# Four projections at 512 weight columns in two halves of rows, and the scan's multiplication on VectorE

## The chip, the cores and the metric

One Trainium2 chip, one core. The metric is the device time of one execution in microseconds (us). The kernel before took 2485.04 us, the median of 3 runs (2484.7 to 2485.36).

## What is computed

One layer of an encoder, on two groups of tokens with shared weights: the sample group S (512 tokens) and the prompt group R (1024 tokens), width 1024, float32.

```python
u = rmsnorm(x, p['mix_norm_g']) @ p['w_in']
ssd_out = ssd_mixer(u[..., OFF_Z:OFF_XBC], u[..., OFF_XBC:OFF_DT], u[..., OFF_DT:OFF_Q], ...)
att_out = attention_mixer(u[..., OFF_Q:OFF_K], u[..., OFF_K:OFF_V], u[..., OFF_V:IN_COLS], ...)
h = x + jnp.concatenate([ssd_out, att_out], axis=-1) @ p['w_out']
h = h + memory_cross_attention(rmsnorm(h, p['xatt_norm_g']), rmsnorm(mem, p['mem_norm_g']), ...)
hm = rmsnorm(h, p['mlp_norm_g'])
y = h + jnp.square(jax.nn.relu(hm @ p['mlp_w1'])) @ p['mlp_w2']
```

`ssd_mixer` holds two chunked scans (one in each direction, 8 heads of 64, chunks of 128 tokens) behind a convolution and a gate z; `attention_mixer` has three banded patterns over 8 heads; `memory_cross_attention` attends to 256 memory tokens of each group, whose keys and values come from `memn @ wkv`.

## The kernel before

**Dense products.** Activations lie transposed in SBUF, each as a high part and a low part (`chi`, `clo`), and so do the weights (`whi`, `wlo`); a product is three matmuls, hi by hi, hi by lo, lo by hi (`mm3`, L198, so L199 to L201). In the four projections of this change (gate z, query/key/value, the memory's keys and values, w_out) and in the cross attention's query the tokens are the stationary operand (128 x 128) and the weights stream: `proj` (L272) makes one tile of 128 tokens by 256 columns with 8 k-steps of three matmuls, 24 matmuls of 256 columns. The convolution's projection, the MLP and the attention's output projection stream 512 columns.

**Weights.** `load_w` (L179) brings a slab of 128 x 2048 values in four pieces of 256 KB: a DMA to `raw` (4 buffers), a cast on ScalarE to `whi`, and a subtraction to `wlo`, on GpSimd for pieces 0 and 2, on VectorE for 1 and 3. The pool `wp` has three buffers each of `whi` and `wlo`, so a slab can be loaded while two others are in use. `slab` (L194) loads 1024 rows by 256 columns.

**The scan.** `ssd` first runs backward over the chunks, then forward. For a chunk and a group of heads `weigh` (L619) makes four 128 x 128 weight tiles in `se`: ScalarE and VectorE steps for each head (L623 to L626), one exponential over 128 x 512 (L627), and one multiplication of 128 x 512 by the exponentials on GpSimd (L628). `inside` (L631) multiplies on TensorE with these tiles (L635). There are 24 such multiplications, 8 for S and 16 for R.

**Order.** Generators of dense work are woven with one chain of mixers (scan S, attention S, scan R, attention R): `weave` (L1130) lets the mixers take `rate` steps for each yield of the dense work. A scheduler that orders the instructions of each engine then fixes the final order when the program is built; at run time each engine works through its own order and waits by semaphore. PSUM: three banks `mm` for projections (`mm_bank`), two `tp`, three for the mixers.

Of the kernel before, what the change touches and what calls it, by code (L numbers as in the profile page):

```python
# [84 lines left out]
def encoder(ctx: ExitStack, tc: tile.TileContext, I, y_p, y_s):  # L85
# [93 lines left out]
    def load_w(src, a, b):  # L179

        hi = wp.tile([128, a, b], F32R, name="whi")
        lo = wp.tile([128, a, b], F32R, name="wlo")

        for s in range(4):
            raw = wp.tile([128, 2, 256], F32, name="raw", bufs=4)
            sl = slice(s * 2, s * 2 + 2) if a == 8 else slice(0, 2)
            sc = slice(0, 256) if a == 8 else slice(s * 256, s * 256 + 256)
# [84 lines left out]
    def proj(w, quads, t):  # L272
# [6 lines left out]
        return ps  # L279

# [19 lines left out]
    def w_in(st, pool, wx, first=False):  # L300
# [67 lines left out]
        def gates(b):  # L368
            for c in range(2):
                if b == 0:  # L370
                    wz.append(slab(W_IN, OFF_Z + c * 256))
                yield from gate(c, wz[c], range(b * 4, b * 4 + 4, 2))

        def gate(c, w, ts):
            for t in ts:
                th = pool.tile([128, 512], F32, name="ev").rearrange("p (t c) -> p t c", t=2)
                for i in range(2):
                    if i:
                        yield
                    ps = proj(w, at, t + i)  # L380
                    nc.scalar.activation(th[:, i], ps, AF.Tanh, scale=0.5)
                    nc.vector.scalar_tensor_tensor(th[:, i], th[:, i], 1.0, ps, op0=OP.add, op1=OP.mult)  # L382
                dst = st.zs[t * 128:t * 128 + 256, c * 256:c * 256 + 256]
                nc.sync.dma_start(dst.rearrange("(t p) c -> p t c", p=128), th)
                catch_up()
                yield
# [64 lines left out]
    def w_in_qkv(st, pool, rot, mid=None):  # L451
# [7 lines left out]
        def heads(c, t, hl):  # L459

            qk = c // 2
            e, sq = f(hl[1]).rearrange("p (t c) -> p t c", t=2), f(hl[0])
            x = e.rearrange("p t (h e) -> p t h e", h=4)
            x3 = e.rearrange("p t (h e) -> p (t h) e", h=4)
            nc.scalar.activation(sq, e.rearrange("p t c -> p (t c)"), AF.Square)
# [3 lines left out]
            nc.vector.tensor_tensor(x3, x3, r[:, :8, None].to_broadcast([128, 8, 64]), op=OP.mult)  # L469
            t1, t2 = x[..., 0:8], x[..., 8:16]  # L470
            m = sq[:, 0:256].rearrange("p (j t h c) -> p j t h c", j=4, t=2, h=4)
            for j, src in enumerate((t1, t2, t1, t2)):
                w = rot[qk][:, t:t + 2, j, None, :].to_broadcast([128, 2, 4, 8])
                (nc.gpsimd if j % 2 else nc.vector).tensor_tensor(m[:, j], src, w, op=OP.mult)
# [3 lines left out]
        def transposed(c, t, hl):  # L478
            qk = c // 2
            e = f(hl[1]).rearrange("p (t c) -> p t c", t=2)  # L480
            pt = tp_bank()
            for hp in range(2):
                for i in range(2):
                    o = (hp * 2 + i) * 128
                    nc.tensor.transpose(pt[:, o:o + 128], e[:, i, hp * 128:hp * 128 + 128], perm)
# [9 lines left out]
        order = [(c, t) for c in range(4) for t in range(0, nt, 2)]  # L495
        order += [(c, b * 4 + t) for b in range(nt // 4) for c in (4, 5) for t in (0, 2)]
        ws = {}
        for c, t in order:
            if c not in ws:
                ws[c] = slab(W_IN, OFF_Q + c * 256)  # L500
            w = ws[c]
            if mid and (c, t) == (4, 4):
                mid()
            if True:
                hl = [pool.tile([128, 512], F32R, name="ev") for _ in range(2 if c < 4 else 1)]
                e = f(hl[-1]).rearrange("p (t c) -> p t c", t=2)
                for i in range(2):
                    if i:
                        yield
                    ps = proj(w, st.at, t + i)  # L510
                    nc.scalar.copy(e[:, i], ps)
                if behind:
                    transposed(*behind.pop())
                if c < 4:
                    heads(c, t, hl)
                    behind.append((c, t, hl))
                else:
                    for i in range(2):
                        for g in range(2):
                            r0 = 64 + (t + i) * 128 + g * 64  # L520
                            dst = st.vd[r0:r0 + 64, (c - 4) * 256:(c - 3) * 256]
                            nc.sync.dma_start(dst.rearrange("(r j) c -> j r c", r=4), e[g * 64:g * 64 + 64, i, :])
                yield


    def ssd(st, pool):
# [92 lines left out]
        def weigh(c, g, cbm, e):  # L619
# [8 lines left out]
            nc.gpsimd.tensor_tensor(w, w, e[:, 0], op=OP.mult)  # L628
# [254 lines left out]
    def memory(pool, late=None):  # L883
        for c in range(8):
            w = slab(WKV, c * 256)
            if late and c == 4:
                late()
            for st in (S, R):
                need("mem" + st.tag)
                kf = pool.tile([128, 512], F32, name="ev").rearrange("p (m c) -> p m c", m=2)  # L890
                ss = pool.tile([128, 2], F32, name="kss", bufs=2)
                for mt in range(2):
                    if mt:
                        yield
                    ps = proj(w, st.mt[:1], st.mt[1] + mt)
                    nc.scalar.copy(kf[:, mt], ps)
                    if c < 4:
                        nc.scalar.activation(ps, ps, AF.Square, accum_out=ss[:, mt:mt + 1])
                hl = [pool.tile([128, 2, 256], F32R, name="ev") for _ in range(2)]
                if c >= 4:  # L900
                    nc.vector.tensor_copy(hl[0], kf)
                    nc.gpsimd.tensor_tensor(hl[1], kf, f(hl[0]), op=OP.subtract)
                    for j in range(2):
                        nc.sync.dma_start(st.v[:, c - 4, j], f(hl[j]).rearrange("p m c -> p (m c)"))
                    yield
                    continue
                r = rstd(pool, ss, 2, 256)
                pt = tp_bank().rearrange("p (e m) -> p e m", e=2)
                for mt in range(2):
                    nc.vector.tensor_scalar(kf[:, mt], kf[:, mt], r[:, mt:mt + 1], None, op0=OP.mult)  # L910
                    for e in range(2):
# [348 lines left out]
```

## Time and profile before

| what | before |
|---|---|
| median of 3 runs | 2485.04 us |
| the profiled execution, device time | 2483.99 us |
| its span, first to last instruction | 2481.9 us |
| TensorE busy (matmuls) | 2413.2 us, 97% |
| VectorE, ScalarE, GpSimd busy | 1416.4, 977.0, 749.0 us |
| mean granted TensorE clock | 0.986 |

The profiled execution lies 1.05 us under the median of the runs. A busy TensorE is one with a matmul in flight: matmuls overlap, each record being longer than the distance to the next, so the rate is read from starts, not from durations. The granted clock is a share of 2.4 GHz; 0.5 of it is 1.2 GHz. Idle time of another engine costs nothing unless TensorE waits for it.

### The profile page before, as it was taken

Reading aid. Unit: us, or ns where it says so; the run is one execution under the profiler, and the core shown is the slowest. Engines: PE = TensorE matmul, PEld = TensorE weight load, DVE = VectorE, ACT = ScalarE, POOL = GpSimd, SP = SyncE. Lnnn points to the kernel's source line nnn. Section 1 sums busy time; section 2 is a strip of 40 time slices with the busy share of each in tenths; the row PEclk is TensorE's granted clock in tenths of the full one; section 3 lists DMA queues with packets and bytes.
Section 4 is the critical chain, followed back from the end, with each engine's and each line's share of the span. In section 5 each row is a group of like instructions: output and inputs, shape, how many; then the busy total and the mean of one; then the engine's idle time right before and its main releaser. Section 6 shows DMA issues by size and latency. Waiting matters only on the chain.

```text
span 2481.9 us, 38736 instructions
## 1 busy us (share of the span) xinstructions
PE 2413.2 (97%) x14435; PEld 2129.5 (86%) x14435; DVE 1416.4 (57%) x2870; ACT 977.0 (39%) x2393; POOL 749.0 (30%) x612
## 2 busy tenths in 40 slices
PE   8899999999899998999999999999999999999999
PEld 6899789998798997888888899999888888888887
DVE  7676876658866566565655636555634434444344
ACT  6445455545544555444433325333521211212111
POOL 3253313425654212332424212111222222322221
PEclk9999999999899999999999999999999999999999
DMA  5555344547675344335335511111111111111111
GB/s 182 182 191 172 121 138 144 169 135 256 226 256 161 87 124 117 105 107 134 107 95 179 181 45 50 54 52 52 35 44 42 52 52 34 54 49 51 51 34 68
DMA packets 258603, 272.28 MB, mean 110 GB/s; under 512 B 43474, under 2 KB 222960, under 8 KB 258416
## 3 DMA queue, kind: packets, MB, share of 16 engines
q1 hardware_dynamic: 258416, 269.82, 35.2%
q8 instruction: 114, 1.87, 0.3%
q14 instruction: 73, 0.60, 0.1%
HBM read 215.55 MB, written 54.20 MB: 109 GB/s over the span
## 4 chain that ended last, share of the span: by engine, by line
PE 73%; DMA 3%; DVE 3%; issue 1%; ACT 1%; POOL 1%; SPq 0%; ACTq 0%; POOLq 0%; DVEq 0%
PE mm L199 15%; PE mm L201 14%; PE mm L200 14%; PE tp L199 7%; PE tp L200 7%; PE tp L201 7%; PE mc L800 2%; PE ma L771 1%; PE mb L787 1%; PE tp L218 1%; DMA se<-acp 1%; DVE se L626 1%; PE mc L635 0%; DMA ak<-qkp 0%; PE tp L981 0%
## 5 line engine op out<-in xcount | busy, mean ns | idle before, releaser
L191 POOL TENSOR_TENSOR wlo<-raw,whi 128x512 fp32r<-128x512 f32 x240 | 364.9, 1537 | 550.3 <-ACT whi L189 451.2
L199 PE MATMUL mm<-whi,chi 128*128 128x256 f32 x1792 | 521.1, 292 | 2.3 <-DVE ev L382 1.7
L201 PE MATMUL mm<-whi,clo 128*128 128x256 f32 x1792 | 511.6, 288 | 1.3 <-DVE clo L225 1.2
L200 PE MATMUL mm<-wlo,chi 128*128 128x256 f32 x1792 | 511.6, 286 | 0.0
L1112 DVE TENSOR_TENSOR h<-mm,h 128x512 f32<-128x512 f32 x384 | 262.5, 688 | 380.7 <-PE mm L201 380.4
L191 DVE TENSOR_TENSOR wlo<-raw,whi 128x512 fp32r<-128x512 f32 x240 | 296.7, 1250 | 97.1 <-ACT whi L189 96.2
L199 PEld LDWEIGHTS mm<-whi,chi 128*128 128x128 f32 x1792 | 344.6, 192 | 5.0 <-DVE ev L382 2.4
L189 ACT CAST whi<-raw 128x512 fp32r<-128x512 f32 x480 | 265.2, 618 | 203.8 <-PE tp L200 100.3
L200 PEld LDWEIGHTS mm<-wlo,chi 128*128 128x128 f32 x1792 | 344.3, 192 | 0.8
L201 PEld LDWEIGHTS mm<-whi,clo 128*128 128x128 f32 x1792 | 342.2, 192 | 2.3 <-DVE clo L225 2.2
L199 PE MATMUL mm<-whi,hidh 128*128 128x512 f32 x768 | 304.2, 396 | 0.0
L201 PE MATMUL mm<-whi,hidl 128*128 128x512 f32 x768 | 303.1, 395 | 0.0
L200 PE MATMUL mm<-wlo,hidh 128*128 128x512 f32 x768 | 302.6, 394 | 0.0
L200 PE MATMUL tp<-clo,whi 128*128 128x512 f32 x720 | 284.4, 395 | 0.0
L199 PE MATMUL tp<-chi,whi 128*128 128x512 f32 x720 | 284.3, 395 | 0.0
L201 PE MATMUL tp<-chi,wlo 128*128 128x512 f32 x720 | 284.0, 394 | 0.0
L1096 POOL TENSOR_TENSOR hidl<-hr,hidh 128x512 fp32r<-128x512 f32 x96 | 124.6, 1298 | 475.7 <-ACT hidh L1095 302.6
L1095 ACT CAST hidh<-hr 128x512 fp32r<-128x512 f32 x96 | 59.6, 621 | 401.1 <-PE mm L200 325.7
L201 PEld LDWEIGHTS mm<-whi,hidl 128*128 128x128 f32 x768 | 144.4, 188 | 33.6
L200 PEld LDWEIGHTS mm<-wlo,hidh 128*128 128x128 f32 x768 | 144.6, 188 | 32.3
L199 PEld LDWEIGHTS mm<-whi,hidh 128*128 128x128 f32 x768 | 144.5, 188 | 32.2
L201 PEld LDWEIGHTS tp<-chi,wlo 128*128 128x128 f32 x720 | 135.4, 188 | 31.1
(284 smaller groups left out, 4132.7 us busy)
## 6 DMA issues: line engine op xcount, KB each, us to landing
raw<-in_mlp_w_dram SPq DMA_DIRECT2D x256, 256.0 KB
raw<-in_w_in_dram SPq DMA_DIRECT2D x96, 256.0 KB
qkp<-ev SPq DMA_DIRECT2D x32, 256.0 KB
raw<-in_xatt_wkv_dram SPq DMA_DIRECT2D x32, 256.0 KB
se<-acp SPq DMA_DIRECT2D x16, 512.0 KB
raw<-in_w_out_dram SPq DMA_DIRECT2D x32, 256.0 KB
raw<-in_xatt_wq_dram SPq DMA_DIRECT2D x32, 256.0 KB
ak<-qkp SPq DMA_DIRECT2D x32, 256.0 KB
```

Source lines behind the costliest of these rows:

```text
L189: nc.scalar.copy(hi[:, sl, sc], raw)
L191: eng.tensor_tensor(lo[:, sl, sc], raw, f(hi[:, sl, sc]), op=OP.subtract)
L199: nc.tensor.matmul(ps, lh, rh, start=start, stop=False)
L200: nc.tensor.matmul(ps, lh, rl, start=False, stop=False)
L201: nc.tensor.matmul(ps, ll, rh, start=False, stop=stop)
L218: nc.tensor.transpose(pt[:, k, t, :], xn[t][:, (2 * kp + k) * 128:(2 * kp + k + 1) * 128], units(2 * kp + k))
L626: nc.vector.scalar_tensor_tensor(w[:, h], cbm[:, 0, g], col[2], w[:, h], op0=OP.mult, op1=OP.add)
L771: nc.tensor.matmul(pq[:, i, :W], qu, ops[i][0][j], start=j == 0, stop=j == 1)
L800: nc.tensor.matmul(po[:, i * 64:i * 64 + 64], pT[:, i * nk + j, :], ops[i][1][j][:, rs], start=j == 0, stop=j == nk - 1)
L1095: nc.scalar.copy(hh[:, ft], r)
L1096: nc.gpsimd.tensor_tensor(hl[:, ft], r, f(hh[:, ft]), op=OP.subtract)
L1112: nc.vector.tensor_tensor(h[t][:, cs], ps, h[t][:, cs], op=OP.add)
```

## The change

`wide_slab` takes 512 columns at once, as two halves of 512 rows, each a slab of its own in `wp`. `wide_proj` makes two tiles of 128 tokens by 512 columns at a time: both take the four k-steps of one half, then the four of the other, and the next pair of tiles begins with the half that was used last. The evictions of the four projections are rewritten for 512 columns of one tile where there were 256 columns of two. `weigh` multiplies on VectorE, the values' low parts are subtracted on VectorE from PSUM (before: a cast on VectorE and a subtraction on GpSimd). Six rates of `weave` change.

```diff
@@ load_w
+        r, c = {8: (2, 256), 4: (1, 512), 2: (2, 256)}[a]
         for s in range(4):
-            raw = wp.tile([128, 2, 256], F32, name="raw", bufs=4)
+            raw = wp.tile([128, 512], F32, name="raw", bufs=4).rearrange("p (r c) -> p r c", r=r)
...
+    def wide_slab(w, c0):
+
+        src = w[:, c0:c0 + 512].rearrange("(u k p) c -> u p k c", p=128, k=4)
+        return [load_w(src[u], 4, 512) for u in range(2)], [0]
...
+    def wide_proj(w, quads, tiles, each):
+
+
+        halves, last = w
+        for t0 in tiles[::2]:
+            ps = [mm_bank() for _ in range(2)]
+            for n in range(2):
+                u = last[0] if n == 0 else 1 - last[0]
+                wh, wl = halves[u]
+                for i in range(2):
+                    hi, lo = quads[(t0 + i) // 4]
+                    ts = slice((t0 + i) % 4 * 128, (t0 + i) % 4 * 128 + 128)
+                    for k in range(4):
+                        kk = u * 4 + k
+                        mm3(ps[i], hi[:, kk, ts], lo[:, kk, ts], wh[:, k, :], wl[:, k, :],
+                            n == 0 and k == 0, n == 1 and k == 3)
+                    if n == 1:
+                        each(t0 + i, ps[i])
+                    yield
+            last[0] = 1 - last[0]
...
+        def gate(t, ps):
+            th = pool.tile([128, 512], F32, name="ev")
+            nc.scalar.activation(th, ps, AF.Tanh, scale=0.5)
+            nc.vector.scalar_tensor_tensor(th, th, 1.0, ps, op0=OP.add, op1=OP.mult)
+            nc.sync.dma_start(st.zs[t * 128:t * 128 + 128, :], th)
...
-                dst = st.qk[qk, (c % 2) * 2:(c % 2) * 2 + 2, j, :, t * 128:t * 128 + 256]
-                nc.sync.dma_start(dst.rearrange("h p t -> p h t"), f(hl[j]).rearrange("p (h t) -> p h t", h=2))
+                dst = st.qk[qk, :, j, :, t * 128:t * 128 + 128]
+                nc.sync.dma_start(dst.rearrange("h p t -> p h t"), f(hl[j]).rearrange("p (h t) -> p h t", h=4))
...
+        for part, each in enumerate((query_key(0), query_key(1), value)):
+            w = wide_slab(W_IN, OFF_Q + part * 512)
+            for b in range(nt // 4):
+                if mid and part == 2 and b == 1:
+                    mid()
+                yield from wide_proj(w, st.at, range(b * 4, b * 4 + 4), each)
@@ weigh
-            nc.gpsimd.tensor_tensor(w, w, e[:, 0], op=OP.mult)
+            nc.vector.tensor_tensor(w, w, e[:, 0], op=OP.mult)
@@ memory
+        def values(st, c, t, ps):
+            hl = [pool.tile([128, 512], F32R, name="ev") for _ in range(2)]
+            nc.scalar.copy(hl[0], ps)
+            nc.vector.tensor_tensor(hl[1], ps, f(hl[0]), op=OP.subtract)
...
-                if c >= 4:
-                    nc.vector.tensor_copy(hl[0], kf)
-                    nc.gpsimd.tensor_tensor(hl[1], kf, f(hl[0]), op=OP.subtract)
@@ w_out
+        for c in range(2):
+            w = wide_slab(W_OUT, c * 512)
+            cs = slice(c * 512, c * 512 + 512)
+            for pr in range(st.nt // 2):
+                need("mix%d%s" % (pr, st.tag))
+                yield from wide_proj(w, st.mixT, range(pr * 2, pr * 2 + 2), each)
@@ the weaving
-        weave(mixing, 0.3, marked(w_in_qkv(S, pool, rot), "qkv s"))
+        weave(mixing, 0.4, marked(w_in_qkv(S, pool, rot), "qkv s"))
-        weave(mixing, 0.45, marked(w_in(R, pool, wx), "w_in p"), 1.0)
+        weave(mixing, 0.5, marked(w_in(R, pool, wx), "w_in p"), 1.0)
-        weave(mixing, 0.9, marked(w_in_qkv(R, pool, rot, memories), "qkv p"), 1.0)
+        weave(mixing, 1.0, marked(w_in_qkv(R, pool, rot, memories), "qkv p"), 1.0)
-        weave(mixing, 0.6, chain(S, (atA,), hp, tp_only), 2.0)
+        weave(mixing, 0.7, chain(S, (atA,), hp, tp_only), 2.0)
-            weave(mixing, 0.65, mlp(S, hid, ready))
+            weave(mixing, 0.5, mlp(S, hid, ready))
```

How this moves instructions, in the order of two engines. TensorE at the first columns of w_out for S, before: the end of one tile of tokens (`mm_8948`) and the beginning of the next (`mm_8974`) on one slab (`whi_8930`, `wlo_8931`).

```order
L199 MATMUL mm_8948<-whi_8930,chi_8103 128x256
L200 MATMUL mm_8948<-wlo_8931,chi_8103 128x256
L201 MATMUL mm_8948<-whi_8930,clo_8104 128x256
L199 MATMUL mm_8974<-whi_8930,chi_8103 128x256
L200 MATMUL mm_8974<-wlo_8931,chi_8103 128x256
L201 MATMUL mm_8974<-whi_8930,clo_8104 128x256
```

And now: the second tile (`mm_7413`) ends with the first half of the rows (`whi_7376`), and the first tile (`mm_7412`) takes the second half (`whi_7394`).

```order
L205 MATMUL mm_7413<-whi_7376,chi_6799 128x512
L206 MATMUL mm_7413<-wlo_7377,chi_6799 128x512
L207 MATMUL mm_7413<-whi_7376,clo_6800 128x512
L205 MATMUL mm_7412<-whi_7394,chi_6799 128x512
L206 MATMUL mm_7412<-wlo_7395,chi_6799 128x512
L207 MATMUL mm_7412<-whi_7394,clo_6800 128x512
```

The matmuls of 512 columns stand where there were two of 256, and an accumulation stays open over both halves.

GpSimd before, from the scan of R beside the loading of w_out's slabs (`wlo_9273`): the multiplication of `se` (L628) stands in one queue with the subtractions of the weights (L191) and of the memory's values (L902).

```order
L647 TENSOR_TENSOR sy_8725<-sy_8725,syo_8792 128x512
L628 TENSOR_TENSOR se_8740<-se_8740 128x512
L628 TENSOR_TENSOR se_8786<-se_8786 128x512
L902 TENSOR_TENSOR ev_8859<-ev_8804,ev_8858 128x512
L191 TENSOR_TENSOR wlo_9273<-raw_9274,whi_9272 128x512
```

VectorE now, at the same stage (scan of R, `wlo_7395` is the second half of w_out's first columns):

```order
L638 SCALAR_TENSOR_TENSOR se_6848<-scbm_6845,dtp_2636,se_6848 128x128 x4
L707 TENSOR_SCALAR sy_6774<-sy_6774,rsr_6966 128x512
L640 TENSOR_TENSOR se_6848<-se_6848 128x512
L192 TENSOR_TENSOR wlo_7395<-raw_7400,whi_7394 128x512
L192 TENSOR_TENSOR wlo_7395<-raw_7408,whi_7394 128x512
L231 SCALAR_TENSOR_TENSOR clo_6800<-tp_7281,cols_81,chi_6799 128x256
```

The multiplication (L640) has moved into VectorE's queue, ahead of w_out's subtractions.

## Rows read from the trace of the kernel before

**Rows 1.** The page: span, busy time by engine, 40 slices.

```profile
PE 2413.2 (97%) x14435; PEld 2129.5 (86%) x14435; DVE 1416.4 (57%) x2870; ACT 977.0 (39%) x2393; POOL 749.0 (30%) x612
...
PE   8899999999899998999999999999999999999999
...
DVE  7676876658866566565655636555634434444344
```

**Rows 2.** TensorE timeline near 1660 us, 256 columns: first and last of 43 rows.

```profile
1659.31 0.28 PE L201 MATMUL mm<-whi,clo 128*128 128x256 f32 x1
...
1664.35 0.29 PE L201 MATMUL mm<-whi,clo 128*128 128x256 f32 x1
```

**Rows 3.** TensorE timeline near 2300 us, 512 columns: first and last of 61 rows.

```profile
2289.84 0.40 PE L200 MATMUL tp<-clo,whi 128*128 128x512 f32 x1
...
2303.79 0.39 PE L200 MATMUL mm<-wlo,hidh 128*128 128x512 f32 x1
```

**Rows 4.** Groups of TensorE by shape: xcount | busy us, mean ns | idle before, releaser.

```profile
L200 PE MATMUL mm<-wlo,chi 128*128 128x256 f32 x1792 | 511.6, 286 | 0.0
```

**Rows 5.** Stretches: length, busy PE PEld DVE ACT POOL, clock, DMA share, GB/s.

```profile
571.00:684.00 113.00, 98.27 (x684) 92.16 (x682) 100.78 (x202) 67.75 (x204) 69.13 (x57) 0.91 0.71 232
684.00:724.00 40.00, 40.00 (x338) 39.85 (x337) 23.34 (x40) 16.99 (x42) 23.13 (x17) 1.00 0.69 228
```

**Rows 6.** Waits of TensorE in 571 to 684 us: total, times, longest.

```profile
PE mc L635 <- POOL se L628: 9.7, 4, 4.3
PE tp L912 <- DVE ev L910: 3.0, 3, 1.1
```

**Rows 7.** Groups of VectorE and GpSimd in 571 to 684 us.

```profile
L626 DVE SCALAR_TENSOR_TENSOR se<-scbm,dtp,se 128x128 f32<-128x128 f32 x44 | 21.2, 534 | 0.4 <-ACT se L625 0.4
L624 DVE SCALAR_TENSOR_TENSOR se<-se,sa 128x128 f32<-128x128 f32 x41 | 17.2, 470 | 2.4 <-ACT se L623 2.4
L191 DVE TENSOR_TENSOR wlo<-raw,whi 128x512 fp32r<-128x512 f32 x10 | 11.8, 1208 | 2.3 <-ACT whi L189 2.1
L575 DVE TENSOR_TENSOR sxs<-sx,sdd 128x512 f32<-128x512 f32 x9 | 6.7, 749 | 0.0
...
L628 POOL TENSOR_TENSOR se<-se 128x512 f32<-128x512 f32 x11 | 14.8, 1342 | 14.2 <-ACT se L625 3.8 <-issue 3.7 <-ACT se L627 2.9
```

**Rows 8.** VectorE and GpSimd timelines around the longest of these waits.

```profile
663.12 5.29 POOL L191 TENSOR_TENSOR wlo<-raw,whi 128x512 fp32r<-128x512 f32 x2 [1.70 <-ACT whi L189]
668.37 1.31 POOL L628 TENSOR_TENSOR se<-se 128x512 f32<-128x512 f32 x1
...
665.92 4.42 DVE L626 SCALAR_TENSOR_TENSOR se<-scbm,dtp,se 128x128 f32<-128x128 f32 x5
```

**Rows 9.** All uses of `se`: duration ns min/median/max, first and last start.

```profile
L626 DVE SCALAR_TENSOR_TENSOR se<-scbm,dtp,se x64: 335/342/1389, 580.8 to 761.3; 128x128 f32<-128x128 f32 x64
```

**Rows 10.** VectorE and GpSimd over the span: the values' steps, and a like subtraction from PSUM.

```profile
L901 DVE CAST ev<-ev 128x512 fp32r<-128x512 f32 x8 | 5.9, 732 | 2.9 <-DMA vp<-ev 1.4 <-ACT ev L896 1.1 <-issue 0.3
L984 DVE TENSOR_TENSOR xqT<-tp,xqT 128x512 fp32r<-128x512 f32 x24 | 16.4, 683 | 3.8 <-ACT xqT L983 3.8
L902 POOL TENSOR_TENSOR ev<-ev 128x512 fp32r<-128x512 f32 x8 | 11.8, 1481 | 11.5 <-DVE ev L901 8.5 <-issue 2.3 <-POOL wlo L191 0.7
```

**Rows 11.** One slab's conversion in the MLP, timelines of ScalarE, GpSimd and VectorE.

```profile
2301.20 2.19 ACT L189 CAST whi<-raw 128x512 fp32r<-128x512 f32 x4 [6.68 <-PE tp L200]
2301.95 3.00 POOL L191 TENSOR_TENSOR wlo<-raw,whi 128x512 fp32r<-128x512 f32 x2 [8.06 <-ACT whi L189]
2304.32 1.18 DVE L191 TENSOR_TENSOR wlo<-raw,whi 128x512 fp32r<-128x512 f32 x1
```

More of the change, by code (lines that the diff above doesn't have):

```diff
@@ L368, in gates @@
         def gates(b):
[L369 to L386, printed above, removed]
+            if b == 0:
+                wz.append(wide_slab(W_IN, OFF_Z))
+            yield from wide_proj(wz[0], at, range(b * 4, b * 4 + 4), gate)
+        def gate(t, ps):
[3 more added lines that the diff above has]
+            nc.sync.dma_start(st.zs[t * 128:t * 128 + 128, :], th)
+            catch_up()
         def steps(_):
@@ L457, in w_in_qkv, with heads @@
         nc.sync.dma_start(st.vd[T + 64:T + 128, :], zero)
[L459 to L465, printed above, removed]
+        def heads(qk, t, hl):
+            e, sq = f(hl[1]), f(hl[0])
+            x = e.rearrange("p (h e) -> p h e", h=8)
+            nc.scalar.activation(sq, e, AF.Square)
             ss = pool.tile([128, 8], F32, name="qss", bufs=2)
@@ L496, in w_in_qkv, with query_key, each @@
[L496 to L511, printed above, removed]
+        def query_key(qk):
+            def each(t, ps):
+                hl = [pool.tile([128, 512], F32R, name="ev") for _ in range(2)]
+                nc.scalar.copy(f(hl[1]), ps)
@@ L512, in w_in_qkv @@
                 if behind:
                     transposed(*behind.pop())
[L514 to L522, printed above, removed]
@@ L523, in w_in_qkv, with value @@
-                yield
+                heads(qk, t, hl)
+                behind.append((qk, t, hl))
+            return each
+        def value(t, ps):
+            e = pool.tile([128, 512], F32, name="ev")
+            nc.scalar.copy(e, ps)
+            if behind:
+                transposed(*behind.pop())
+            for g in range(2):
+                r0 = 64 + t * 128 + g * 64
+                dst = st.vd[r0:r0 + 64, :]
+                nc.sync.dma_start(dst.rearrange("(r j) c -> j r c", r=4), e[g * 64:g * 64 + 64, :])
@@ L917, in memory, with each @@
-                for j in range(2):
-                    nc.sync.dma_start(st.kt[:, c, j], f(hl[j]).rearrange("p e m -> p (e m)"))
-                yield
+                held = []
+                def each(t, ps):
+                    if c > 1:
+                        if behind:
+                            keys(*behind.pop(0))
+                        return values(st, c * 2 - 4, t, ps)
+                    mt = t % 2
+                    for h in range(2):
+                        if mt == 0:
+                            kf = pool.tile([128, 512], F32, name="ev").rearrange("p (m c) -> p m c", m=2)
+                            held.append((st, c * 2 + h, kf, pool.tile([128, 2], F32, name="kss", bufs=6)))
+                        _, _, kf, ss = held[h]
+                        cs = slice(h * 256, h * 256 + 256)
+                        nc.scalar.copy(kf[:, mt], ps[:, cs])
+                        nc.scalar.activation(ps[:, cs], ps[:, cs], AF.Square, accum_out=ss[:, mt:mt + 1])
+                    if mt:
+                        behind.extend(held)
+                    for _ in range(len(behind) - 1):
+                        keys(*behind.pop(0))
@@ L922, in mix_T @@
+                yield from wide_proj(w, st.mt[:1], range(st.mt[1], st.mt[1] + 2), each)
     def mix_T(st, pr, atp, banks=(tp_bank,)):
@@ L946, in w_out, with each @@
             st.h.append(x)
-        ws = {}
-        order = [(c, t) for c in range(2) for t in range(st.nt)]
-        order += [(c, pr * 2 + t) for pr in range(st.nt // 2) for c in (2, 3) for t in range(2)]
-        for c, t in order:
-            if c not in ws:
-                ws[c] = slab(W_OUT, c * 256)
-            if c == 0 and t % 2 == 0:
-                need("mix%d%s" % (t // 2, st.tag))
-            ps = proj(ws[c], st.mixT, t)
-            hs = st.h[t][:, c * 256:c * 256 + 256]
+        def each(t, ps):
+            hs = st.h[t][:, cs]
             nc.vector.tensor_tensor(hs, ps, hs, op=OP.add)
-            if c == 3 and t % 2:
+            if cs.start and t % 2:
                 done(t // 2)
-            yield
+        for c in range(2):
[4 more added lines that the diff above has]
+                yield from wide_proj(w, st.mixT, range(pr * 2, pr * 2 + 2), each)
     def xattn(st, xk, xp, bank, done):
```

70 lines of the change are left out of this document (31 added, 39 removed).

## The prediction

> **What bounds the kernel now.** I read the page first: TensorE has a matmul in flight in 97% of the span, VectorE is at 57%, and the forty slices show the same TensorE level nearly everywhere, with dips at the start and around slices 10 to 15, where VectorE's digits are highest [rows 1]. So a gain must make TensorE's stream shorter or take away one of the few stretches in which it stalls. Then I read the rate of that stream from its timeline, since busy times overlap. In a dense run of 256 columns, 43 starts lie between 1659.31 and 1664.35 us: 5.04 / 42 = 0.1200 us each [rows 2]. In a dense run of 512 columns, 61 starts lie between 2289.84 and 2303.79 us: 13.95 / 60 = 0.2325 us each [rows 3]. Last I read the worst stall. From 571 to 684 us (the memory's projection beside the scan of R) TensorE is busy for 98.3 of 113 us at a granted clock of 0.91, which means about a fifth of the stretch at 1.2 GHz: 14.7 us idle plus (1 - 0.91) x 113 = 10.2 us of slow clock, 25 us lost. VectorE is busy for 100.8 of the 113 us there, 89% [rows 5]. Two thirds of that idle time end with the scan's multiplication on GpSimd: 9.7 us in 4 waits [rows 6].
>
> **The wider stream.** There are 3 x 1792 matmuls of 256 columns with these operands [rows 4]. The query keeps 4 slabs x 12 tiles x 24 = 1152. The four projections hold the rest: (24 for z + 72 for query, key, value + 32 for the memory + 48 for w_out) x 24 = 4224, which become 2112 of 512 columns; the order shows them in that form. Each pair becomes one and saves 2 x 0.1200 - 0.2325 = 0.0075 us, in all 2112 x 0.0075 = **15.8 us** [rows 2, 3]. It lies on TensorE, which nothing covers, except where something else sets the pace. The memory's 32 x 24 / 2 = 384 pairs run mostly in the stretch just described, so I give back 384 x 0.0075 = 2.9 us. **-12.9 us.** The bounds are 0 (all of it turns into waiting) and -15.8.
>
> The Trainium skill speaks for less: "TensorE: Matmul & The Clock Gate", section "Back-to-back issue gap", gives a warm matmul N / 2.4 + 2.5 ns, that is 109.2 ns at 256 columns and 215.8 ns at 512, so a pair would save 2.5 ns and 2112 pairs 5.3 us. This trace has the larger distances, 120.0 and 232.5 ns, and with them the larger saving; I take the trace.
>
> **Fewer, wider evictions.** Where 256 columns of two tiles were evicted by two instructions, 512 of one tile are evicted by one. ScalarE and VectorE get lighter by fixed costs, which TensorE does not wait for: 0. A tile now holds its bank over both halves, but a bank is wanted again only after about two more half tiles of 12 matmuls (24 x 0.2325 = 5.6 us), where before it was two more tiles of 24 (48 x 0.1200 = 5.8 us). The query's and key's stores go out in 512-byte runs instead of 1024, those of z and of the values in 2048, the weights come in 2048: the same bytes, off the path: 0. If this cover failed, a late store would hold an `ev` buffer and, behind it on ScalarE, an eviction.
>
> **Reloading a half.** A slab now needs two of the three buffers, so the next slab's second half must wait for a half to come free. In the order the shortest such way is in w_out for S: 33 matmuls of 512 columns stand between the last on the old content and the first on the new, 33 x 0.2325 = 7.7 us. The conversion itself took from 2301.20 to 2305.50 us in the MLP, 4.3 us [rows 11]. I take 0; the bounds are 0 and 1 us for each of 16 wide slabs (one for z and three for query, key and value in each group, four for the memory, two for w_out in each group), if ScalarE, GpSimd or VectorE comes to it 4.4 us late. What would wait behind such a cast on ScalarE are the scan's exponentials, and behind them TensorE's L635.
>
> **The multiplication on VectorE.** GpSimd loses 24 of 1.34 us, 11 of them in the bad stretch [rows 7], and 8 subtractions of 1.48 us [rows 10]. What the wait costs is seen in one case: GpSimd subtracts two pieces of weights from 663.12 to 668.41 us and comes to `se` only at 668.37, done at 669.68 [rows 8]. Without GpSimd's queue up to 9.7 us of waits go, and with them up to 10.2 us of slow clock that follow such pauses [rows 5, 6]. But VectorE's own steps of the next weight tile run until 670.34 in the same place [rows 8]: VectorE is the next to be late. **I take -6 us**, between 0 and -19.9.
>
> Against that, VectorE gets the multiplication. It never ran there; the nearest rows of 128 x 512 from SBUF with two tensors are 0.75 us (`sxs`) and 1.21 us (the weights' subtraction) [rows 7]. I take 0.75, the nearest in kind, a product of two SBUF tensors by the same scan in the same stretch: 11 x 0.75 = 8.2 us in a stretch where VectorE is 89% busy, so all of it counts; the bound is 11 x 1.21 = 13.3 us. The other five of R fall behind 684 us, where VectorE is busy for 23.3 of 40 us [rows 5], and the eight of S where its digits are 6 to 8 of ten [rows 1]: 0. In return VectorE is held up less: `se` steps took 0.534 and 0.470 us in this stretch, while the median of the former is 0.342 us [rows 7, 9], so 44 x 0.192 + 41 x 0.128 = 13.7 us were lost beside GpSimd; GpSimd's load there falls by 14.8 of 69.1, 21%, and 2.9 us come back. The values' cast (0.73 us) goes from VectorE and a subtraction from PSUM (0.68 us by a like one) comes [rows 10]: 0. **+5 us**, between -3 and +13.
>
> The Trainium skill says of this contention ("SBUF — State Buffer", section "SBUF: two separate sides") that a VectorE instruction with two SBUF inputs and a GpSimd instruction exclude each other for their whole length. The trace agrees as far as it goes: five `se` steps took 4.42 us beside GpSimd's subtractions, against 5 x 0.34. By that rule the moved multiplication is itself such an instruction, and would be held by the weights' subtractions of up to 2.6 us that it is meant to escape.
>
> **The sum.** 2484.0 us of the profiled execution - 12.9 - 6 + 5 = 2470.1; the median of the runs lies 1.05 us above the profiled one: **2471 us**. A measurement can tell about 0.2%, 5 us, from no change.
>
> **Rivals.**
>
> *The bad stretch grows (slower).* The rates of weaving rise, so more of R's scan is pushed into the same place: between w_out's first subtraction and the query's first, VectorE's order has 47 rows on `se` where it had 32. With the scan's other rows that is some 18 us more work, on top of 58% of about 50 us [rows 5]: 47 of 50. If w_out then stalls as the memory's stretch does (25 of 113, so 11 us of 50), the multiplications cost 19.4 us (16 x 1.21) and nothing comes back from GpSimd, it is 2484.0 - 12.9 + 11 + 19.4 + 1 = **2503**. It decides once VectorE is over 90% busy behind the memory's stretch too. For it speaks that VectorE is already the limit next to TensorE there; against it, that GpSimd's queue, not VectorE's, ended most of the idle time [rows 6].
>
> *Halves come late (no change).* 2471 + 16 x 1 = **2487**. For it: ScalarE, VectorE and GpSimd serve the scan in the same queues, and the margin of 7.7 - 4.3 us is smaller than one chunk's weights. Against it: the MLP lives with 4.3 us conversions and never stalls [rows 1, 11].
>
> *Only the fixed part of the rate is saved (no change).* The distances of 0.1200 and 0.2325 us come from different stages, and each may contain something of its stage (the loading of other tensors, the two banks in turn). If a pair saves 2.5 ns, the first term is -5.3 and the time **2482**. Against it: both runs are steady over 40 and more starts. That the change leaves the width as it was can be excluded: the order shows the 512 columns.
>
> *GpSimd was the whole stall (faster).* If the four waits and the pauses' slow clock were all due to GpSimd's queue, the 25 us go at no charge: 2484.0 - 15.8 - 25 + 1 = **2444**. Against it: VectorE at 89%.
>
> **How the numbers follow.** The forecast has a chance of 0.50, and its own range is 2459 to 2480: the two terms of the multiplication half way to their bounds either way (-7 and -2 to +3 and +4) and the first at -12.9 to -15.8. The growing stretch has 0.18, the late halves 0.12, the smaller rate gain 0.05, the vanishing stall 0.15. Faster by over 0.2%: nearly all of the forecast and the last, 0.63. Within 0.2%: 0.12 + 0.05 and an edge of the forecast, 0.19. Slower: 0.18. The range of 8 in 10 leaves out the dearer half of the growing stretch and the better half of the vanishing stall: 2449 to 2497.
>
> **What would show it.** Right: starts of the four projections 0.232 us apart; no wait of TensorE on GpSimd for `se`, a few on VectorE; between 15 and 25 us lost in the stretch of the memory's projection. Wrong: TensorE waiting for `whi` or `wlo` at the turns of the halves; VectorE over 90% busy with TensorE idle in w_out for S; projection starts at other distances.

## The result, and the profile after

| | median of the runs | lowest to highest | profiled execution | its span |
|---|---|---|---|---|
| before | 2485.2 us (4 runs) | 2484.7 to 2485.39 | 2483.99 us | 2481.9 us |
| after | 2457.19 us (4 runs) | 2453.35 to 2460.61 | 2460.61 us | 2458.8 us |

The ratio is 0.9887, with a 95% interval of 0.987 to 0.9904: faster by 28 us in the medians. The two profiled executions lie 23.4 us apart; the forecast had 13.9 between them. The changed kernel's own runs spread over 7 us, and the profiled one is the slowest of the four, 3.4 us above their median.

The changed kernel's page answers to [rows 1]: engines first (busy us, share, instructions), then slices.

```profile
PE 2394.6 (97%) x12323; PEld 2008.7 (82%) x12323; DVE 1412.9 (57%) x2858; ACT 967.1 (39%) x2337; POOL 709.6 (29%) x580
...
PE   8998999999889999999999999999999999999999
...
DVE  7777676648985567566564635555534344444444
```

TensorE has 14435 - 12323 = 2112 matmuls fewer, as counted ahead, and is busy 18.6 us less; VectorE has what it had. Those two figures don't say where the time went. I split each profiled span in three: **idle** (span less TensorE's busy time), **clock loss** (one less the granted clock, times the span) and the **rest** (busy time less clock loss), which is the length of the stream itself, at full clock, as far as records that overlap can give it. The clock is known to 0.001, that is to some 1.2 us either way in a loss.

| kernel | median us | ratio to before, 95% | span | busy PE | clock | idle | clock loss | rest |
|---|---|---|---|---|---|---|---|---|
| before | 2485.2 | 1 | 2481.9 | 2413.2 | 0.986 | 68.7 | 34.7 | 2378.5 |
| after | 2457.19 | 0.987 to 0.9904 | 2458.8 | 2394.6 | 0.991 | 64.2 | 22.1 | 2372.5 |
| a_again | 2457.18 | 0.9865 to 0.9901 | 2456.6 | 2396.4 | 0.990 | 60.2 | 24.6 | 2371.8 |
| a_split256 | 2451.52 | 0.9846 to 0.9873 | 2447.9 | 2394.2 | 0.996 | 53.7 | 9.8 | 2384.4 |
| a_split_cols | 2455.93 | 0.9861 to 0.9893 | 2454.8 | 2401.0 | 0.994 | 53.8 | 14.7 | 2386.3 |
| a_mixed | 2450.8 | 0.9844 to 0.9877 | 2450.3 | 2392.8 | 0.995 | 57.5 | 12.3 | 2380.5 |
| a_split_slabs | 2466.99 | 0.9909 to 0.9943 | 2461.0 | 2403.6 | 0.992 | 57.4 | 19.7 | 2383.9 |
| a_old_rates | 2469.87 | 0.9923 to 0.995 | 2465.0 | 2400.7 | 0.988 | 64.3 | 29.6 | 2371.1 |
| a_pool_mult | 2461.57 | 0.9876 to 0.9912 | 2459.8 | 2397.8 | 0.991 | 62.0 | 22.1 | 2375.7 |
| a_one_tile | 2453.69 | 0.9859 to 0.9885 | 2448.1 | 2391.5 | 0.992 | 56.6 | 19.6 | 2371.9 |
| a_no_turns | 2443.49 | 0.9822 to 0.9849 | 2446.8 | 2391.4 | 0.992 | 55.4 | 19.6 | 2371.8 |
| a_narrow_evict | 2455.1 | 0.9866 to 0.9892 | 2453.7 | 2388.9 | 0.993 | 64.8 | 17.2 | 2371.7 |
| b_new_rates | 2481.83 | 0.9975 to 0.9994 | 2482.6 | 2410.4 | 0.989 | 72.2 | 27.3 | 2383.1 |
| b_dve_mult | 2485.28 | 0.9992 to 1.001 | 2480.5 | 2410.2 | 0.987 | 70.3 | 32.2 | 2378.0 |

From before to after the columns give 6.0 us to the stream, 4.5 to idle time and 12.6 to clock loss. But these columns count slow clock that falls into idle time twice, and the rest comes out too short by as much. By the clock's own records in the traces, the loss while TensorE is busy is 28.2 us before and 19.9 after. With that the stream goes from 2385.0 to 2374.7: of the 23.1 us between the spans the stream gives 10.3, idle time 4.4 and the clock 8.3. So rather more than half of the gain is not the wider stream. Where the waiting went is read from stretches (length, then busy time of PE, PEld, DVE, ACT, POOL, then clock, DMA share, GB/s). Before:

```profile
0.00:130.00 130.00, 110.69 (x655) 97.14 (x656) 89.31 (x180) 68.10 (x141) 41.82 (x40) 0.96 0.60 186
130.00:550.00 420.00, 410.20 (x2999) 385.00 (x2999) 283.98 (x737) 213.92 (x549) 147.45 (x145) 0.98 0.49 149
550.00:1000.00 450.00, 417.89 (x2997) 392.72 (x2996) 314.65 (x688) 241.11 (x666) 182.90 (x149) 0.95 0.57 175
```

After:

```profile
0.00:130.00 130.00, 118.06 (x535) 94.96 (x536) 93.81 (x188) 71.17 (x141) 44.80 (x45) 1.00 0.62 196
130.00:550.00 420.00, 404.41 (x2079) 334.40 (x2078) 283.99 (x732) 210.94 (x513) 136.10 (x134) 0.98 0.49 148
550.00:1000.00 450.00, 418.67 (x2493) 363.73 (x2492) 324.08 (x779) 251.65 (x720) 151.82 (x126) 0.97 0.60 182
```

Idle and clock loss together: the first 130 us fall from 19.3 + 5.2 = 24.5 to 11.9 + 0 us (**-12.6**); 130 to 550 rises from 18.2 to 24.0 (+5.8); 550 to 1000 falls from 54.6 to 44.8 (-9.8). (With a clock of two digits the losses of the two long stretches are good to some 2 us each. Counted only while TensorE is busy, the first 130 us fall by 11.5.)

**The first 130 us** were in no term. Before, TensorE stands still for a load of the scan of S (`sbt`), then for an eviction buffer, and then runs at the lower clock (start, length, line and operation):

```profile
87.20 2.04 PE L582 MATMUL ma<-sxs,sbt 128*128 128x256 f32 x4 [5.32 <-DMA sbt<-bts]
90.97 0.58 PE L199 MATMUL mm<-whi,chi 128*128 128x256 f32 x1 [1.73 <-DVE ev L382]
...
91.78 0.41 PE L199 MATMUL mm<-whi,chi 128*128 128x256 f32 x1
...
96.90 0.39 PE L199 MATMUL mm<-whi,chi 128*128 128x256 f32 x1
```

From 91.78 to 96.90 us lie 24 distances of 5.12 / 24 = 0.213 us, where the same matmuls take 0.120 at full clock [rows 2]. The stretch from 82 to 97 us as a whole:

```profile
82.00:97.00 15.00, 8.07 (x32) 7.20 (x33) 9.24 (x22) 6.70 (x19) 2.59 (x2) 0.66 0.70 217
```

That is 6.9 us idle and 0.34 x 15 = 5.1 us of clock; 1.0 us of the latter falls into the pauses, which leaves 11 us lost in 15. In the same 15 us after, TensorE is busy throughout at full clock. The same product is far later in its order now. The lines are all products with `sbt` (durations in ns, first and last start), before and then after:

```profile
L582 PE MATMUL ma<-sxs,sbt x80: 377/379/764, 87.2 to 763.1; 128*128 128x256 f32 x80
```

```profile
L594 PE MATMUL ma<-sxs,sbt x80: 377/379/634, 117.5 to 707.8; 128*128 128x256 f32 x80
```

The load is issued at 85.0 us before and at 84.4 after; only TensorE's first use moved, from 87.2 to 117.5, and the wait is gone. By the records of the two traces 348 matmuls stand ahead of that product before and 476 after, with wider matmuls among them.

**The memory's projection**, the bad stretch of the prediction, after (compare [rows 5]):

```profile
560.00:673.00 113.00, 101.25 (x486) 81.34 (x485) 101.40 (x206) 67.28 (x198) 52.55 (x44) 0.96 0.75 246
673.00:724.00 51.00, 44.12 (x213) 35.49 (x211) 41.73 (x90) 26.48 (x72) 22.76 (x18) 0.97 0.79 262
```

In 113 us 11.8 are idle and 4.5 are clock loss: 16.3 us where it was 25. The same program in another execution (a_again) loses 12.6 + 6.8 = 19.3 us there:

```profile
560.00:673.00 113.00, 100.45 (x474) 80.87 (x473) 98.16 (x204) 66.31 (x196) 51.77 (x44) 0.94 0.77 243
```

VectorE is busy for 101.4, 90%, as it was. TensorE's waits for the multiplication are now on VectorE (total, times, longest), in 560 to 724 us and in 724 to 742:

```profile
PE mc L647 <- DVE se L640: 7.0, 6, 2.1
...
PE mc L647 <- DVE se L640: 5.4, 1, 5.4
```

The longest one ends at 725.68 us, and it goes back to a load. The rows of `se` are brought by DMA (L628 of SyncE's queue, issued among the loads of w_out's weights). ScalarE is idle for 8.8 us until they are there, VectorE for 7.3 us until ScalarE has done its first step, and the multiplication (L640) is the end of that chain:

```profile
712.31 0.38 SPq L628 DMA_DIRECT2D se<-acp  x1
...
720.37 1.27 ACT L635 ACTIVATE se<-se,sa 128x128 f32<-128x128 f32 x4 [8.77 <-DMA se<-acp]
...
720.80 1.23 DVE L636 SCALAR_TENSOR_TENSOR se<-se,sa 128x128 f32<-128x128 f32 x4 [7.34 <-ACT se L635]
...
724.90 0.68 DVE L640 TENSOR_TENSOR se<-se 128x512 f32<-128x512 f32 x1
...
725.68 1.94 PE L647 MATMUL mc<-sx,se 128*128 128x64 f32 x8 [5.41 <-DVE se L640]
```

So this wait is put down to VectorE only because VectorE's step came last. In a_again ScalarE waits for the same load, 6.3 us until 716.47, and TensorE's wait at that place is 2.9 us. No run moves this load, so what it is worth is not shown.

### The profile page after: what moved, and what is told of

The parts are those of the page before. It is cut to its first block, busy times and chain, and to the rows that moved or that the text cites. A ratio compares the mean times of both kernels' runs of the same rounds, so it can differ in the third digit from the quotient of the medians.

```text
span 2458.8 us, 34311 instructions
## 1 busy us (share of the span) xinstructions
PE 2394.6 (97%) x12323; PEld 2008.7 (82%) x12323; DVE 1412.9 (57%) x2858; ACT 967.1 (39%) x2337; POOL 709.6 (29%) x580
## 3 DMA queue, kind: packets, MB, share of 16 engines
q8 instruction: 97, 1.59, 0.3%
## 4 chain that ended last, share of the span: by engine, by line
PE 69%; DMA 5%; DVE 4%; issue 2%; ACT 1%; POOL 1%; SPq 1%; POOLq 0%; ACTq 0%; DVEq 0%
PE mm L205 13%; PE mm L207 13%; PE mm L206 13%; PE tp L205 7%; PE tp L207 7%; PE tp L206 7%; PE mc L812 2%; PE ma L783 1%; PE mb L799 1%; DMA se<-acp 1%; PE tp L224 1%; DVE wlo L192 1%; DMA raw<-in_xatt_wq_dram 1%; DVE se L638 0%; POOL wlo L192 0%
## 5 line engine op out<-in xcount | busy, mean ns | idle before, releaser
L205 PE MATMUL mm<-whi,chi 128*128 128x512 f32 (+1 forms) x1088 | 398.0, 366 | 6.7 <-ACT chi L230 3.7
L206 PE MATMUL mm<-wlo,chi 128*128 128x512 f32 (+1 forms) x1088 | 392.9, 362 | 0.0
L207 PE MATMUL mm<-whi,clo 128*128 128x512 f32 (+1 forms) x1088 | 391.6, 363 | 0.0
L205 PEld LDWEIGHTS mm<-whi,chi 128*128 128x128 f32 x1088 | 207.8, 191 | 36.2 <-ACT chi L230 5.0
L207 PEld LDWEIGHTS mm<-whi,clo 128*128 128x128 f32 x1088 | 206.7, 190 | 28.8
L206 PEld LDWEIGHTS mm<-wlo,chi 128*128 128x128 f32 x1088 | 207.5, 191 | 27.3
```

The costliest lines, as they stand in the source:

```text
L205: nc.tensor.matmul(ps, lh, rh, start=start, stop=False)
L206: nc.tensor.matmul(ps, lh, rl, start=False, stop=False)
L207: nc.tensor.matmul(ps, ll, rh, start=False, stop=stop)
```

## The experiments

Each kernel was timed beside the kernel before on the same chip, whose medians there were 2485.3, 2486.2 and 2485.8 us. Three theories are weighed: (A) the wider stream is the gain; (B) waits are, and the width is not; (C) it is the order into which the parts fall.

**a_again**, the changed kernel once more.

> The changed kernel, run again beside its variants. It took 2457.2 us in 4 runs (2453.4 to 2460.6) against 2485.2 before. Both theories (the rate of the wide stream; stalls that shrank) expect 2453 to 2461; it is the level from which the variants of this group are read.

2457.18 us (2451.91 to 2462.49). The result repeats; 5 us to either side is this kernel's own spread.

**a_split256**, everything of the change but the width:

```diff
-                        mm3(ps[i], hi[:, kk, ts], lo[:, kk, ts], wh[:, k, :], wl[:, k, :],
-                            n == 0 and k == 0, n == 1 and k == 3)
+                        for h in range(2):
+                            cc = slice(h * 256, h * 256 + 256)
+                            mm3(ps[i][:, cc], hi[:, kk, ts], lo[:, kk, ts], wh[:, k, cc], wl[:, k, cc],
+                                n == 0 and k == 0 and h == 0, n == 1 and k == 3 and h == 1)
```

> The changed kernel with every matmul of the four projections cut in two of 256 columns again (same slabs, halves, evictions, engines). If the rate is what the change is worth, 2112 x 0.0075 = 15.8 us come back: 2470 to 2476, with projection starts 0.120 us apart. If only 2.5 ns per pair are saved: 2460 to 2464. If the gain came from stalls, loads and evictions: 2455 to 2461.

2451.52 us (2449.73 to 2453.2): not slower by the stream's gain, but 5.7 us faster than the change (the two intervals, 0.9846 to 0.9873 and 0.987 to 0.9904, just overlap, so only "not slower" is safe). Its rest is 2384.4, 12.3 us more than in after and a_again, so the stream does get longer; its idle time and clock loss are 63.5 us where those have 85 to 86. The gain of the width is there, and as much or more comes back as waiting. Theory A falls as an account of the net time.

**a_split_cols**: as a_split256, but with the loop over column halves outside the k-steps.

```diff
+                    for h in range(2):
+                        cc = slice(h * 256, h * 256 + 256)
+                        for k in range(4):
```

> As the cut kernel of 256 columns (2451.5), but the four k-steps of the first 256 columns stand ahead of those of the second, so the order differs while the number of matmuls and their rate stay. If shorter matmuls as such let the mixers' matmuls in sooner and save some 22 us of waiting: 2448 to 2455 again. If the cut kernel had a lucky order: 2460 or more, 15.8 us of rate on top of the changed kernel's stalls, up to 2473.

2455.93 us (2452.23 to 2456.64): rest 2386.3, idle and clock loss 68.5. One microsecond outside the range named for shorter matmuls as such. Same width, another order: 4.4 us, with intervals that overlap.

**a_mixed**: 512 columns in w_out of R alone, where no mixer runs beside it; 256 in the other stages.

```diff
-                yield from wide_proj(w, st.mixT, range(pr * 2, pr * 2 + 2), each)
+                yield from wide_proj(w, st.mixT, range(pr * 2, pr * 2 + 2), each, 1 if st is R else 2)
```

> Matmuls of 256 columns in the four projections while mixers run beside them, 512 columns in w_out for the prompt group, where none runs. There the changed kernel took 108.0 us from the first projection matmul to the query's first transpose, before it was 110.7 and in the cut kernel 111.4. If the rate is real where nothing else is late: 3 us less than the cut kernel, 2448 to 2449, and 108 us in that stretch. If the rate is given back: 2451 to 2452.

2450.8 us (2448.32 to 2454.49): 6 us under the change (the intervals touch), level with a_split256. The 3 us that the width brings in that stage can't be told from noise in the time. They can be read in the traces: w_out of R from its first matmul to the query's first transpose, with 256 columns (a_split256) and with 512 (a_mixed) on the same slabs.

```profile
1376.79 0.37 PE L205 MATMUL mm<-whi,chi 128*128 128x256 f32 x1
...
1488.16 0.60 PE L1009 MATMUL tp<-ident,xq 128*128 128x128 f32 x4
```

```profile
1382.49 0.48 PE L205 MATMUL mm<-whi,chi 128*128 128x512 f32 x1
...
1490.48 0.49 PE L1009 MATMUL tp<-ident,xq 128*128 128x128 f32 x3
```

111.37 and 107.99 us, 3.4 us, as expected. The same stretch before and after:

```profile
1411.48 0.37 PE L199 MATMUL mm<-whi,chi 128*128 128x256 f32 x1
...
1522.19 0.49 PE L981 MATMUL tp<-ident,xq 128*128 128x128 f32 x3
```

```profile
1390.94 0.48 PE L205 MATMUL mm<-whi,chi 128*128 128x512 f32 x1
...
1498.92 0.49 PE L1007 MATMUL tp<-ident,xq 128*128 128x128 f32 x3
```

110.71 and 107.98 us: 2.73 us for 2 x 8 x 24 = 384 pairs, 0.0071 us each, where 0.0075 was forecast. In the same stretch of after 62 starts lie at 0.2325 us (14.18 / 61), the distance of [rows 3]:

```profile
1419.68 0.40 PE L205 MATMUL mm<-whi,chi 128*128 128x512 f32 x1
...
1433.86 0.39 PE L206 MATMUL mm<-wlo,chi 128*128 128x512 f32 x1
```

**a_old_rates**: the five weaving rates of before (five rates differ, not six as said ahead).

```diff
-        weave(mixing, 0.4, marked(w_in_qkv(S, pool, rot), "qkv s"))
+        weave(mixing, 0.3, marked(w_in_qkv(S, pool, rot), "qkv s"))
...
-            weave(mixing, 0.5, mlp(S, hid, ready))
+            weave(mixing, 0.65, mlp(S, hid, ready))
```

> The changed kernel with the five old weaving rates. If the new rates push too much of the scan of R into the memory's stretch (the rival that ends slower), the old ones make it 5 to 15 us faster; if they matter to the start of the scan of S (a wait of 5.3 us on its load, gone after the change), 5 to 10 us slower; if they are worth nothing, within 4 us.

2469.87 us (2466.78 to 2472.58), 12.7 us slower than the change, no overlap. On this code the rates are worth that much; the rest is unchanged (2371.1), clock loss is 29.6. New waits of TensorE stand in attention and scan:

```profile
PE ma L783 <- DMA aq<-qkp: 5.8, 1, 5.8
PE ma L594 <- ACT carry L598: 4.7, 1, 4.7
```

**b_new_rates**: the kernel before with the new rates alone.

> The kernel before with the five new rates and nothing else. On the changed kernel they are worth 12.7 us: if they are worth as much here, 2472.5. If the rates pay only with the new slabs: 2483 to 2490, or more if they push the scan of R into a stretch where GpSimd is late.

2481.83 us (2477.64 to 2488.02), ratio 0.9985: about 4 us. The same numbers that bring 12.7 us with the new slabs bring a third of it without.

**a_split_slabs**: the halves, the evictions and the values' subtraction alone: 256 columns as in a_split256, the old rates, the multiplication on GpSimd.

> Only the slabs in two halves, the wider evictions and the values on VectorE: 256 columns, old rates, the multiplication on GpSimd. If the parts add up (rates 12.7, multiplication 4.4 as measured on the changed kernel): 2451.5 + 17.1 = 2468.6. If the loads and evictions are the whole gain: 2452 to 2457. If they are worth nothing: 2483 to 2487.

2466.99 us (2461.66 to 2472.15), 19.2 us faster than before at an unchanged width. The largest piece of the change is one that the prediction had at 0. Its first 130 us and its products with `sbt`:

```profile
0.00:130.00 130.00, 117.22 (x747) 104.39 (x747) 90.91 (x179) 68.83 (x134) 43.99 (x43) 1.00 0.59 185
```

```profile
L596 PE MATMUL ma<-sxs,sbt x80: 377/379/631, 132.9 to 742.9; 128*128 128x256 f32 x80
```

12.8 us lost there instead of 24.5: 11.7 of the 19.2. (The rest was not followed, and the three parts of this kernel were not timed one by one; a_narrow_evict below takes up the evictions.) The wait for `sbt` is there in all three kernels with the old slabs (first product at 87.2, 86.5 and 86.7 us), and in none of the eleven with the new (117.5 to 132.9). So the new slabs, with the order of tiles that goes with them, take that wait away, whatever the rates, the width and the engine of the multiplication.

**a_pool_mult**: the multiplication back on GpSimd.

```diff
-            nc.vector.tensor_tensor(w, w, e[:, 0], op=OP.mult)
+            nc.gpsimd.tensor_tensor(w, w, e[:, 0], op=OP.mult)
```

> The changed kernel with the scan's multiplication back on GpSimd. My sum (-6 for GpSimd's queue, +5 for VectorE's load) expects it 1 us slower than the changed kernel, within 5. If GpSimd's queue was the whole stall: 15 us or more slower, with waits of TensorE on GpSimd of 10 us and over. If VectorE's load is the limit: some 8 us faster, VectorE less than 90% busy in the stretch of the memory's projection.

2461.57 us (2454.02 to 2464.26): 4.4 us slower, with intervals that overlap. In the memory's stretch it loses somewhat more:

```profile
560.00:673.00 113.00, 99.11 (x456) 79.39 (x457) 99.30 (x197) 64.85 (x191) 64.53 (x54) 0.92 0.72 232
```

13.9 idle and 9.0 of clock, 22.9 us against 16.3 in after and 19.3 in a_again; the medians differ by 4.4.

**b_dve_mult**: the same edit on the kernel before, alone.

> The kernel before with the scan's multiplication on VectorE and nothing else changed. My forecast's terms give -6 for GpSimd's queue and +5 for VectorE's load: 2481 to 2487. If GpSimd was the whole stall of the memory's stretch, 2460 to 2470. If VectorE's load takes the wait's place and more, 2490 or above. On the changed kernel the same edit was worth about 4 us, not clear of the noise; parts that add up would give 2481.

2485.28 us (2480.9 to 2489.99), ratio 1.0001 with 0.9992 to 1.001: nothing. The wait only changes its engine, from 9.7 us on GpSimd [rows 6] to

```profile
PE mc L635 <- DVE se L628: 8.4, 3, 4.7
```

So GpSimd's queue alone was not the stall; the rival of the vanishing stall falls.

**a_narrow_evict**: every eviction of 512 columns issued as two of 256.

```diff
-                nc.scalar.copy(f(hl[1]), ps)
+                for cc in (slice(0, 256), slice(256, 512)):
+                    nc.scalar.copy(f(hl[1])[:, cc], ps[:, cc])
```

> The changed kernel with every eviction of 512 columns of z, query, key, value, the memory's values and w_out issued as two of 256: 56 more ScalarE instructions and 44 more VectorE ones, some 0.16 us of engine time each. If the fewer evictions are what the new slabs bring (about 18 us at unchanged width), 2468 to 2478. If they were rightly costed at nothing, 2452 to 2463.

2455.1 us (2453.06 to 2457.17): no slower, with 56 and 44 instructions more. Fewer evictions bring nothing by themselves that can be told from the noise.

**a_one_tile**: a tile takes both halves, then the next tile; no pairs, no turns.

```diff
-        for t0 in tiles[::2]:
-            ps = [mm_bank() for _ in range(2)]
-            for n in range(2):
+        for t in tiles:
+            ps = mm_bank()
+            for u in range(2):
```

> The changed kernel with the tiles of the four projections made one after the other: one tile takes the four k-steps of the first half and then the four of the second, then the next tile does; no pairs, no turns. The next slab's second half can then begin to load only 12 matmuls (12 x 0.2325 = 2.8 us) before the old slab ends, and a conversion takes 4.3 us. If the halves in turns are what keeps the loads on time, each of some 11 changes from one wide slab to the next costs 1.5 to 3 us: 2474 to 2490, with TensorE waiting for whi or wlo. If loads have enough slack in the third buffer whatever the order, 2452 to 2463 as the changed kernel.

2453.69 us (2449.84 to 2456.49): no slower, though the least way from a half's last use to its successor's first is 2.8 us here. TensorE's whole waiting for weights:

```profile
PE mm L206 <- DVE wlo L192: 0.8, 2, 0.6
```

**a_no_turns**: pairs of tiles, but the halves always first, then second.

```diff
-            last[0] = 1 - last[0]
```

> The changed kernel with the halves always taken first, then second, for every pair of tiles (they do not turn). The least way from the last use of a half to the first use of its successor falls by one half slab use. If the loading of halves was near its limit (my rival of late halves), 2462 to 2475 with waits for whi or wlo; if it has slack, the changed kernel's 2452 to 2463, and the term of 0 for reloading stands.

2443.49 us (2442.24 to 2448.61), ratio 0.9836 (0.9822 to 0.9849): 13.7 us faster than the change, with no overlap, and the fastest kernel of the study. I had expected it to be level at best. Its rest is that of after (2371.8); it idles 55.4 us instead of 64.2. TensorE's waiting for weights is the same 0.8 us:

```profile
PE mm L206 <- DVE wlo L192: 0.8, 1, 0.8
```

Taking turns brings no benefit that any run here shows. Most of the idle time that is saved lies between 130 and 550 us: 7.7 us here, 15.6 in after and 14.8 in a_again. (The profiled execution is the slowest of the four, so it shows less than the medians do.)

```profile
130.00:550.00 420.00, 412.30 (x2127) 342.98 (x2126) 287.77 (x744) 214.84 (x523) 137.05 (x137) 0.98 0.52 155
```

No single wait there in after is longer than 3.2 us, and which row of the order spares them was not followed further.

Of the three theories A falls. a_split256 has the whole gain without the width, so it is one of waits and slow clock (B), and what moves the waits is the order (C): the new slabs, the rates and the turns each change it, and each is worth 13 to 19 us one way or the other.

## Why the prediction was right, and where it was not

The direction and the range held: 2457 lies between 2449 and 2497, but outside the forecast's own 2459 to 2480, by 2 us. The gain of 28 us is twice the 14 that were forecast, and it has other causes. That the number fell into the range is in good part luck: the term that made most of the sum is worth nothing in the time, and two gains that the sum left out came in its place. Two figures of the prediction are not what its own terms give. Half way from +5 to its bound of -3 is -4, not -2, so the forecast's own range would be 2457 to 2478, with the result at its very edge. And the rival of the smaller rate gain comes to 2484.0 - 5.3 - 6 + 5 + 1 = 2479, not 2482. By its own steps:

- **The wider stream, -12.9: nearly right in size, wrong in what it is worth.** Among kernels with the new slabs, those of 256 columns have a rest of 2383.9 to 2386.3 (mean 2384.9), those of 512 one of 2371.1 to 2375.7 (mean 2372.4): 12.5 us. With clock loss counted only while TensorE is busy, and with the kernels on the old slabs, it is 2383.8 to 2387.9 against 2373.9 to 2377.2, 11 us between the means. And the rate of a pair was met, 0.0071 us before to after and 0.0088 (3.38 / 384) on the same slabs. That rate speaks against a saving of 2.5 ns a pair, the estimate from the formula that the Trainium skill gives for isolated matmuls ("TensorE: Matmul & The Clock Gate", "Back-to-back issue gap"), as the first trace did; that rival falls. What failed is the sentence that the gain lies on TensorE, "which nothing covers, except where something else sets the pace", with 2.9 us given back: a_split256, which does without the width and is no slower, shows that all of it is given back. The bound "0 (all of it turns into waiting)" is what the runs show of the term. Whether the shorter matmuls themselves spare the waits or the order that they lead to isn't settled: both kernels of 256 columns with the new rates and the multiplication on VectorE wait less (63.5 and 68.5 us of idle and clock loss) than the five like it of 512 (75.0 to 86.3), but among these five the order alone moves 11.3.
- **Evictions 0 and reloading a half 0: right.** a_narrow_evict, and the waits of 0.8 us in a_one_tile and a_no_turns; in after no wait for `whi` or `wlo` is in the list at all. The rival of late halves falls.
- **The multiplication, -6 and +5: right as a sum.** Alone it is worth 0 and on the changed kernel about 4 us. A multiplication was priced at 0.75 us and takes 0.778 in the mean, 0.672 at least and 1.671 at most:

```profile
L640 DVE TENSOR_TENSOR se<-se 128x512 f32<-128x512 f32 x24 | 18.7, 778 | 0.5
...
L640 DVE TENSOR_TENSOR se<-se x24: 672/679/1671, 152.0 to 733.4; 128x512 f32<-128x512 f32 x24
```

  Three of the 24 took over 1 us (1.67, 1.59 and 1.13), and each began while a GpSimd instruction was running, two of them during subtractions of weights. Three others that began inside such a subtraction took 0.68 us; there GpSimd's subtraction lasted 3.5 and 3.9 us instead of some 1.3. This agrees with the rule of the Trainium skill ("SBUF — State Buffer", "SBUF: two separate sides") that one of the two engines holds up the other; by these records the one that is held is not always the one that began later.

- **What to see in the bad stretch: right.** 16.3 us lost (19.3 in a_again), within the 15 to 25 named (the 25 us of before count 1.8 us of slow clock in the pauses twice); no wait on GpSimd for `se`, seven on VectorE. Of the growing stretch a small part seems to come true: from 673 to 724 us 6.9 are idle and 1.5 are clock loss, 8.4 us, with VectorE at 82%, where 3.4 and 1.4 were lost at the like place before (below). But 3.7 us of that idle time are the beginning of the wait that goes back to the load of `se`, which the prediction did not consider, and not VectorE's load. The rival's point of decision, VectorE over 90%, was not reached, and its 19 us for the multiplications did not come.

```profile
684.00:731.00 47.00, 43.64 (x357) 43.15 (x356) 30.18 (x57) 23.23 (x60) 25.82 (x20) 0.97 0.72 249
```

- **The step that failed is the sum's list itself.** It had one place where a stall could go, the memory's stretch. But the new slabs put TensorE's work into another order, and the largest single gain that was found, 11 us, came at 82 to 97 us, in a wait of 5.3 us for `sbt` that the trace of before showed plainly and that the sum passed over; with the shorter wait and the clock behind it, it weighed about twice its length. That the product with `sbt` stands later in the new order was not weighed ahead either. The rates, too, stood only in a rival, as a harm; on the new code they are worth 12.7 us of gain.

By medians of single edits: slabs, evictions and values -19.2 (a_split_slabs to before), rates -12.7, multiplication -4.4 (unclear), width +5.7 (hardly clear): -30.6 in all against -28.0 measured. They need not add up exactly, since each edit reorders the rest: the rates alone give 4, the multiplication alone 0.

## What to carry to other kernels

A shorter stream on the busiest engine is worth its saving only in stages where that engine sets the pace; try the width stage by stage, and look at idle time and clock loss beside it. Where a scheduler orders the work, an edit is also a new order: list every stall of the old trace (with the clock that it costs behind it) and look up in the new order what stands ahead of each waiting instruction. And leave one part out at a time: here one line less, the turns of the halves, was worth as much as the whole forecast.

## What the runs showed that I had not expected

A pause of 5.3 us and one of 1.7 us close behind it cost some 4 us more through the clock: the loss while TensorE was busy, of which 24 distances of 0.213 us instead of 0.120 make 2.2. That the clock is a second price of waits is seen over the whole span, too: from before to after its loss while TensorE is busy falls by 8.3 us, idle time by 4.4. And kernels with the same matmuls, which differ only in the order of halves and tiles, lie between 2443.5 and 2457.2 us, about 0.6% apart, which is as much as most edits here bring.
